# Two heads' scores and values of three attention branches alternate in pinned runs of matmuls, and the compression sums stand in four column groups

## The chip, the cores and the metric

One core of one Trainium2 chip runs the whole program. The metric is the device time of one execution in microseconds (us). Before the change it was 1890.36 us, the median of 3 runs (1888.82 to 1891.26).

TensorE (PE) multiplies a stationary operand, which it loads first, with a moving one. VectorE (DVE), ScalarE (ACT) and GpSimd (POOL) work beside it, and SyncE (SP) issues the transfers. [...]

## The reference

A decoder of two layers on 256 tokens of width 1024. Each layer has four token mixers, a merge of them, and a channel mixer (a dense SwiGLU in layer 0, eight experts of which each token takes two in layer 1). What the change touches, cut to the core:

```
# A: per head, three groups g of banded attention over 256 keys, mixed by their softmax sums
#    (three groups' exponentials over one common sum)
# C: per query head, three attentions with a sigmoid gate each:
kc = gelu(flat(k_cmp blocks) @ w1[0] + b1[0]) @ w2[0] + b2[0]     # compression, 15 blocks, K = 2048
vc = gelu(flat(v_cmp blocks) @ w1[1] + b1[1]) @ w2[1] + b2[1]
o  = g0*softmax(q kc^T) vc + g1*softmax(q k_slc^T) v_slc + g2*softmax(q k_win^T) v_win
# D: sliding window of 128 keys, 6 query heads on 2 key heads, a learned sink in the denominator
o_d = softmax(q k^T) v * sigmoid(lse - sink)
# each branch (256 x 384) then: merged += sigmoid(x @ w_gate + b) * (branch @ w_branch)
```

## The kernel before, in words

Tokens are handled in two tiles of 128 rows (`t` = 0 and 1), and features in tiles of 128. A head has 64 features, so one feature tile holds two heads: head s = 0 in its rows 0 to 63, s = 1 in rows 64 to 127 (`half`, L267).

**Projections.** Every weight tile (128x1024) is loaded by SP (L77), copied in reduced precision by ACT and completed by a DVE subtraction (`split_into`, L81), and used in 24 matmuls of 256 columns (`mm3`, L95, L97, L103). These go on all through the mixers: q and k for branch A (`z_a`), for the conv, for C and D (`zmm`, `ztile`), then the merge gates (`gates`, L486) and the merges. They read only the layer's input, or branches that are done, so they are the work that fills PE between attention steps.

**Attention.** A unit is one pair of heads `j` and one row tile `t`. It computes scores into a PSUM tile `sc` (two of these exist, 1024 columns each), adds the mask and takes the row extremum (DVE), exponentiates (ACT), takes the reciprocal and scales (DVE), transposes 128x128 blocks on PE (`transposed`, L264), copies them to SBUF as `pt` (ACT), and multiplies them with the values into `po` (one PSUM tile, head s in its rows 64s to 64s+63), which `branch_out` (L232) writes out as two parts. Per layer `attn_a` (L270) has 3 pairs, `attn_c` (L408) 3 and `attn_d` (L305) 3.
In `attn_a` the six score products of t = 0 come head by head (L284), the three of each head at t = 1 in a pass of its own; the value products (L300) come head by head too, with 64 columns of weights. `attn_c` does the same with two score products per head (L425, L426), values of two key sets (L453) and a last product over the 16 compressed blocks (L455), which has 16 rows; these 16 columns are transposed apart (L443) and copied by DVE (L447). `attn_d` issues one score product for each head (L312) and one or two value products for each (L337).

**Compression.** `compress` (L342) sums 16 products of 128x32 weights for k and then 16 for v into 32 partitions (L368), transposes the result in two pieces (L374), and goes on with a gelu.

**Order.** A list scheduler sets each engine's order when the program is built. It takes whatever is ready by its own estimates, so projections stand between attention steps. Before the change nothing binds it in the attention.

Of the kernel before, what the change touches and what calls it, by code (L numbers as in the profile page):

```python
# [41 lines left out]
def build(ctx, tc, d):  # L42
# [121 lines left out]
    with tc.tile_pool(name="psa", bufs=1, space=PSUM) as pa:  # L164
# [4 lines left out]
        def po_ps():  # L169
            return pa.tile([P, 512], F32, tag="po", name="po", bufs=1)  # L170
# [19 lines left out]
        for i in range(DEPTH):  # L190
            with tc.tile_pool(name=f"mix{i}", bufs=1) as mp:
# [77 lines left out]

                def attn_a(j, br):  # L270
                    for t in range(NT):
                        nk = (t + 1) * P
                        n = 3 * nk
                        po = po_ps()
                        mask = (ma0 if t == 0 else ma1).rearrange("p g n -> p (g n)")
                        for heads in (((0, 1),) if t == 0 else ((0,), (1,))):
                            ps = sc_ps()
# [17 lines left out]
                            for b, s in enumerate(heads):  # L295
                                for g in range(3):
                                    for kb in range(t + 1):
                                        c = (g * 6 + 2 * j + s) * 64
                                        o = b * n + g * nk + kb * P
                                        te.matmul(po[half(s), :P], vt[:, kb, c:c + 64], pt[:, o:o + P],  # L300
                                                  start=(g + kb == 0), stop=(g == 2 and kb == t))
                        branch_out(po[:, :P], br[j][0][:, t * P:(t + 1) * P], br[j][1][:, t * P:(t + 1) * P], 0.5)


                def attn_d(br, zq, zk):  # L305
                    for j in range(3):
                        for t in range(NT):
                            nk = (t + 1) * P
                            po = po_ps()
                            ps = sc_ps()  # L310
# [1016 lines left out]
```

## Time and profile before

| | us |
|---|---|
| median of 3 runs | 1890.36 |
| the profiled execution | 1891.61 |
| its span from first to last instruction | 1889.6 |
| PE busy | 1808.7 (96%) |
| PE weight loads busy | 1315.5 (70%) |
| DVE busy | 911.8 (48%) |
| ACT busy | 736.0 (39%) |

The span is 2.0 us short of the execution's own time. PE's busy time counts overlapping matmuls once, and the end of each is modelled. So how many run at once is read from the starts in the timeline, not from the busy share. An fp32 product stands there as two records, a projection or a transpose as one. The first 345 us and those from about 635 to 965 us are the two layers' mixers; the experts' stage runs from about 1010 us to the end.

### The profile page before, as it was taken

How to read it: one execution, taken by the hardware profiler on the slowest of the kernel's cores; microseconds unless marked ns; L12 is line 12 of the kernel's file. 1: busy time of each engine (PE TensorE's matmuls, PEld its weight loads, DVE VectorE, ACT ScalarE, POOL GpSimd, SP SyncE). 2: the span in 40 equal slices, each digit the busy share in tenths (PEclk: the TensorE clock that was granted, in tenths of full speed). 3: DMA queues.
4: the chain of work that ended last, by engine and by line, in shares of the span. 5: the costliest groups of instructions: out<-in, count | busy, mean ns of one | idle time of the engine just before them, and what ended most of it. 6: DMA issues, size and time to landing. Idle time of an engine off the chain costs nothing. (4 is left out here: it accounts for less than half of the span.)

```text
span 1889.6 us, 28149 instructions
## 1 busy us (share of the span) xinstructions
PE 1808.7 (96%) x11091; PEld 1315.5 (70%) x11091; DVE 911.8 (48%) x1565; ACT 736.0 (39%) x1185; POOL 78.1 (4%) x115
## 2 busy tenths in 40 slices
PE   8999999999999999999999999999999998998995
PEld 8998789979998999878997454434554453454341
DVE  5565565767555556555577433313333341333232
ACT  4444554545443344455453333213233241233220
POOL 2000001300001000000220000000000000000000
PEclk9999999999999999999999999999999999999998
DMA  7434235567554334423557999999999999999995
GB/s 252 149 141 161 74 137 183 194 219 256 194 185 161 134 134 157 157 72 115 189 201 300 382 421 421 421 421 421 421 421 421 421 421 421 421 420 421 422 421 211
DMA packets 99516, 524.10 MB, mean 277 GB/s; under 512 B 11696, under 2 KB 12464, under 8 KB 56368
## 3 DMA queue, kind: packets, MB, share of 16 engines
q1 hardware_dynamic: 99376, 522.22, 70.5%
q8 instruction: 89, 1.46, 0.3%
q14 instruction: 51, 0.42, 0.1%
HBM read 519.03 MB, written 3.15 MB: 276 GB/s over the span
## 5 line engine op out<-in xcount | busy, mean ns | idle before, releaser
L81 DVE TENSOR_TENSOR wl<-raw,wh 128x1024 fp32r<-128x1024 f32 (+3 forms) x325 | 396.5, 1227 | 211.6 <-ACT wh L81 163.2
L81 ACT CAST wh<-raw 128x1024 fp32r<-128x1024 f32 (+3 forms) x325 | 329.1, 1020 | 347.8 <-PE mm L97 202.4
L95 PE MATMUL mm<-xth,wh 128*128 128x256 f32 x1472 | 363.7, 285 | 5.8 <-ACT wh L81 5.8
L97 PE MATMUL mm<-xtl,wh 128*128 128x256 f32 x1472 | 361.1, 283 | 0.0
L95 PEld LDWEIGHTS mm<-xth,wh 128*128 128x128 f32 x1472 | 278.8, 189 | 13.5 <-ACT wh L81 6.3
L97 PEld LDWEIGHTS mm<-xtl,wh 128*128 128x128 f32 x1472 | 278.8, 189 | 5.3 <-issue 3.4
L1030 PE MATMUL mm<-mraw,xes 128*64 128x512 f32 x1024 | 238.2, 599 | 13.0 <-DMA mraw<-in_mgu 9.8
L103 PE MATMUL mm<-xth,wl 128*128 128x256 f32 x1472 | 212.3, 283 | 0.0
L103 PEld LDWEIGHTS mm<-xth,wl 128*128 128x128 f32 x1472 | 189.3, 190 | 4.6 <-issue 3.9
L1039 DVE TENSOR_TENSOR hsm<-hsm,mm 64x512 f32<-64x512 f32 x42 | 28.5, 678 | 310.6 <-ACT hsm L1038 310.6
L1030 PEld LDWEIGHTS mm<-mraw,xes 128*64 128x64 f32 x1024 | 67.3, 136 | 151.1 <-issue 118.3
L81 DVE TENSOR_TENSOR wl<-mraw,wh 128x1024 fp32r<-128x1024 f32 x118 | 138.8, 1221 | 41.9 <-ACT wh L81 40.5
L81 ACT CAST wh<-mraw 128x1024 fp32r<-128x1024 f32 x118 | 118.6, 1049 | 41.6 <-DMA mraw<-in_mgu 29.4
L1038 ACT ACTIVATE hsm<-mm 64x512 f32<-64x512 f32 x42 | 24.9, 593 | 272.5 <-PE mm L1030 272.5
L1061 PE MATMUL sc<-mraw,hts 128*64 128x512 f32 x472 | 110.2, 597 | 10.1 <-ACT hsm L1038 3.2
L892 PE MATMUL mm<-wh,xth 128*128 128x512 f32 x224 | 96.5, 431 | 14.9 <-ACT wh L81 14.9
L893 PE MATMUL mm<-wh,xtl 128*128 128x512 f32 x224 | 88.6, 396 | 0.0
L1061 PEld LDWEIGHTS sc<-mraw,hts 128*64 128x64 f32 x472 | 32.0, 136 | 80.7 <-issue 60.7
L501 POOL TENSOR_TENSOR x<-x,gt 128x256 f32<-128x256 f32 x48 | 50.1, 1064 | 665.6 <-DVE gt L499 665.6
L1030 PE MATMUL mm<-raw,xes 128*64 128x512 f32 x320 | 75.3, 599 | 2.4 <-DMA raw<-in_mgu 2.3
L896 PE MATMUL mm<-wl,xth 128*128 128x512 f32 x224 | 71.4, 400 | 0.6
L892 PEld LDWEIGHTS mm<-wh,xth 128*128 128x128 f32 x224 | 42.4, 189 | 35.7 <-ACT wh L81 26.9
(341 smaller groups left out, 2439.4 us busy)
## 6 DMA issues: line engine op xcount, KB each, us to landing
mraw<-in_mgu SPq DMA_DIRECT2D x166, 1024.0 KB, 19.8
mraw<-in_md SPq DMA_DIRECT2D x80, 1024.0 KB, 19.8
raw<-in_mgu SPq DMA_DIRECT2D x58, 1024.0 KB, 19.8
raw<-in_wz SPq DMA_DIRECT2D x75, 512.0 KB, 4.1
raw<-in_wmg SPq DMA_DIRECT2D x64, 512.0 KB, 4.3
raw<-in_md SPq DMA_DIRECT2D x32, 1024.0 KB, 19.8
raw<-in_wv SPq DMA_DIRECT2D x24, 520.0 KB, 4.5
raw<-in_wbr SPq DMA_DIRECT2D x32, 384.0 KB, 3.5
```

Source lines behind the costliest of these rows:

```text
L81: return sc.copy(hi, src), v.tensor_tensor(lo, src, hi.bitcast(F32), ALU.subtract)
L95: te.matmul(ps, ah[asl], bh[bsl], start=first, stop=False)
L97: te.matmul(ps, ah[asl], bl[bsl], start=False, stop=False)
L103: te.matmul(ps, lhs, rhs, start=False, stop=last)
L501: gp.tensor_tensor(merged[j], merged[j], gs[j], ALU.add)
L892: mm(ps, ah[asl], bh[bsl], start=first, stop=False)
L893: mm(ps, al[asl], bh[bsl], start=False, stop=False)
L896: mm(ps, lhs, rhs, start=False, stop=last_)
L1030: mm(ps[HP * s:HP * s + HP], self.xe[:, k], w[s][cols(a * 512, 512)], start=(k == 0), stop=(k == KD - 1))
L1038: sc.activation(h[:HP], ps[HP:], AF.Silu)
L1039: v.tensor_tensor(h[:HP], h[:HP], ps[:HP], ALU.mult)
L1061: mm(self.dn[HP * c:HP * c + HP], ht[:, a], w[cols(c * 512, 512)], start=(n == 0), stop=(n == 4 * NFB - 1))
```

## The change

- `together` (new) issues a list of products and ties each behind the one before it on PE, so that they stand in one run; with `behind` the first is tied to what was traced before it.
- Scores (`attn_a`, `attn_c`, `attn_d`): the products of the two heads alternate, s = 0, 1, 0, 1, in the two row halves, into different banks. At t = 1 both heads' scores come in one run, before either head's softmax. From a unit's second row tile on (in C and D also from the second pair on) they are tied behind the unit before's values.
- Values (`pv`, new): the products of both heads alternate in the two column halves, in one run once both heads' `pt` are there. `po` holds both row tiles of a pair, and `branch_out` runs once per pair on 256 columns.
- `attn_d` takes both row tiles in one unit: one softmax tile, six transposes, one copy.
- `attn_c`: the compressed scores go to tiles `pc` of 128 columns, zero behind the 16, and `vc` gets 128 rows, zero below the 16. So the transposes and the last value product have the shape of the others, ACT copies `pt` with them (640 or 768 columns), and the DVE copy is gone.
- `compress`: four sums of eight products (k and v, two halves each) in four groups of 32 columns, one product of each in turn; all four weight tiles are loaded first. One transpose of 128x128, and DVE adds the halves.
- The tag `zc` has 6 buffers, not 8.

```
+def together(products, behind=False):
+    for n, (out, lhs, rhs, first, last) in enumerate(products):
+        ins = te.matmul(out, lhs, rhs, start=first, stop=last)
+        if n or behind:
+            tc.keep_in_program_order(ins)
+def pv(po, t, blocks):
+    todo = [blocks(s) for s in range(2)]
+    together([(po[half(s), t * P:(t + 1) * P], *todo[s][n], n == 0, n == len(todo[s]) - 1)
+              for n in range(len(todo[0])) for s in (1, 0)])
...
 def attn_a(j, br):
+    po = po_ps()
     for t in range(NT):
         nk = (t + 1) * P
         n = 3 * nk
-        po = po_ps()
         mask = (ma0 if t == 0 else ma1).rearrange("p g n -> p (g n)")
-        for heads in (((0, 1),) if t == 0 else ((0,), (1,))):
-            ps = sc_ps()
+        groups = ((0, 1),) if t == 0 else ((0,), (1,))
+        tiles = [sc_ps() for _ in groups]
+        pss = [tiles[0][:, 512 * s:] if t == 0 else tiles[s] for s in range(2)]
+        together([(pss[s][:, g * nk:(g + 1) * nk], za["q", g, j][half(s), t * P:(t + 1) * P],
+                   za["k", g, j][half(s), :nk], True, True) for g in range(3) for s in range(2)], t > 0)
+        where = {}
+        for heads in groups:
             pe = soft_tile()
             nh = len(heads)
             st = sm(3 * nh)
-            for b, s in enumerate(heads):
-                for g in range(3):
-                    o = 512 * b + g * nk
-                    te.matmul(ps[:, o:o + nk], za["q", g, j][half(s), t * P:(t + 1) * P],
-                              za["k", g, j][half(s), :nk], start=True, stop=True)
             spans = [(b * n, n) for b in range(nh)]
             for b, (o, w) in enumerate(spans):
-                v.tensor_tensor_reduce(pe[:, o:o + w], ps[:, 512 * b:512 * b + w], mask, 1.0, 3e38, ALU.add, ALU.min,
-                                       st[:, b:b + 1])
+                v.tensor_tensor_reduce(pe[:, o:o + w], pss[heads[b]][:, :w], mask, 1.0, 3e38, ALU.add,
+                                       ALU.min, st[:, b:b + 1])
             softmax_rows(pe, st, spans)
             scale_rows(pe, st[:, 2 * nh:], spans)
             pst = transposed(pe, 3 * nh * (t + 1))
             pt = pt_tile()
             sc.copy(pt[:, :nh * n], pst[:, :nh * n])
             for b, s in enumerate(heads):
-                for g in range(3):
-                    for kb in range(t + 1):
-                        c = (g * 6 + 2 * j + s) * 64
-                        o = b * n + g * nk + kb * P
-                        te.matmul(po[half(s), :P], vt[:, kb, c:c + 64], pt[:, o:o + P],
-                                  start=(g + kb == 0), stop=(g == 2 and kb == t))
-        branch_out(po[:, :P], br[j][0][:, t * P:(t + 1) * P], br[j][1][:, t * P:(t + 1) * P], 0.5)
+                where[s] = pt[:, b * n:b * n + n]
+        def blocks(s):
+            return [(vt[:, kb, (g * 6 + 2 * j + s) * 64:(g * 6 + 2 * j + s) * 64 + 64],
+                     where[s][:, g * nk + kb * P:g * nk + (kb + 1) * P])
+                    for g in range(3) for kb in range(t + 1)]
+        pv(po, t, blocks)
+    branch_out(po[:, :S], br[j][0], br[j][1], 0.5)
...
 def attn_d(br, zq, zk):
     for j in range(3):
+        po = po_ps()
+        tiles = [sc_ps() for _ in range(NT)]
+        together([(tiles[t][:, 512 * s:512 * s + (t + 1) * P], zq[j][half(s), t * P:(t + 1) * P],
+                   zk[half(s), :(t + 1) * P], True, True) for t in range(NT) for s in range(2)], j > 0)
+        pe = soft_tile()
+        st = sm(12)
...
+        spans = [(0, P), (P, P), (2 * P, S), (2 * P + S, S)]
...
+        pst = transposed(pe, 6)
+        pt = pt_tile()
+        sc.copy(pt, pst[:, :3 * S])
+        for t in range(NT):
+            pv(po, t, lambda s: [
+                (vt[:, kb, 1408 + s * 64:1408 + s * 64 + 64],
+                 pt[:, spans[2 * t + s][0] + kb * P:spans[2 * t + s][0] + (kb + 1) * P])
+                for kb in range(t + 1)])
+        branch_out(po[:, :S], br[j][0], br[j][1], 0.5)
...
-    for kv in range(2):
-        for half in range(2):
-            w = load(d["w1"][i, kv, half], 1024)
-            for a in range(8):
-                b = 8 * half + a
-                te.matmul(ps[:32, kv * P:(kv + 1) * P], gs[kv][:, b].rearrange("p h c -> p (h c)"),
-                          w[:, a * P:(a + 1) * P], start=(b == 0), stop=(b == 15))
-    hs = stile([32, S], F32, "chs", 1, mp)
-    v.tensor_copy(hs, ps[:32, :S])
+    w = [load(d["w1"][i, n // 2, n % 2], 1024) for n in range(4)]
+    together([(ps[32 * n:32 * n + 32, :P], gs[n // 2][:, 8 * (n % 2) + a].rearrange("p h c -> p (h c)"),
+               w[n][:, a * P:(a + 1) * P], a == 0, a == 7) for a in range(8) for n in (3, 2, 1, 0)])
+    hs = stile([P, P], F32, "chs", 1, mp)
+    v.tensor_copy(hs, ps[:, :P])
...
-    for kv in range(2):
-        te.transpose(ps[:, kv * 32:kv * 32 + 32], hs[:, kv * P:(kv + 1) * P], ident[:32, :32])
+    te.transpose(ps[:, :P], hs, ident)
...
     for kv in range(2):
-        v.tensor_scalar(hx[:, kv * 32:kv * 32 + 32], ps[:, kv * 32:kv * 32 + 32],
-                        pp[:, PP_B1 + kv:PP_B1 + kv + 1], None, ALU.add)
+        c = slice(kv * 32, kv * 32 + 32)
+        v.tensor_scalar(hx[:, c], ps[:, kv * 64:kv * 64 + 32], pp[:, PP_B1 + kv:PP_B1 + kv + 1], None,
+                        ALU.add)
+        v.tensor_tensor(hx[:, c], hx[:, c], ps[:, kv * 64 + 32:kv * 64 + 64], ALU.add)
...
-    vc = stile([16, 2, 64], F32, "vc", 1, mp)
+    vc = stile([P, 2, 64], F32, "vc", 1, mp)
+    v.memset(vc, 0.0)
     for hd in range(2):
-        v.scalar_tensor_tensor(vc[:, hd], psv[:16, hd * 64:hd * 64 + 64], 0.5, b2v[:16], ALU.mult,
+        v.scalar_tensor_tensor(vc[:16, hd], psv[:16, hd * 64:hd * 64 + 64], 0.5, b2v[:16], ALU.mult,
...
+    pcs = [stile([P, 2, P], F32, f"pc{n}", 1, mp) for n in range(2)]
+    for pc in pcs:
+        v.memset(pc, 0.0)
     for j in range(3):
+        po = po_ps()
         for t in range(NT):
             nk = (t + 1) * P
...
             mask = ma0[:, 0, :] if t == 0 else mc1
-            for heads in (((0, 1),) if t == 0 else ((0,), (1,))):
+            groups = ((0, 1),) if t == 0 else ((0,), (1,))
+            tiles = [sc_ps() for _ in groups]
+            pss = [tiles[0][:, 512 * s:] if t == 0 else tiles[s] for s in range(2)]
+            wo = 16 + nk if t == 0 else 512
+            together([(pss[s][:, o:o + w], zq[j][half(s), t * P:(t + 1) * P], z[half(s), :w], True, True)
+                      for z, o, w in ((zw, wo, nk), (zs, 0, 16 + nk)) for s in range(2)],
+                     j + t > 0)
+            where = {}
+            pc = pcs[(j + t) % 2]
+            for heads in groups:
                 nh = len(heads)
...
-                    q = zq[j][half(s), t * P:(t + 1) * P]
-                    so = 512 * b
-                    wo = so + (16 + nk if t == 0 else 512)
-                    te.matmul(ps[:, so:so + 16 + nk], q, zs[half(s), :16 + nk], start=True, stop=True)
-                    te.matmul(ps[:, wo:wo + nk], q, zw[half(s), :nk], start=True, stop=True)
...
+                    for dst, src, w, mk in ((pc[:, s, :16], 0, 16, mcmp[:, t, :]),
+                                            (pe[:, o:o + nk], 16, nk, mask),
+                                            (pe[:, o + nk:o + 2 * nk], wo, nk, mask)):
...
+                pst = transposed(pe, 4)
+                for b, s in enumerate(heads):
+                    te.transpose(pst[:, 512 + b * P:512 + (b + 1) * P], pc[:, s], ident)
                 pt = pt_tile()
-                sc.copy(pt[:, :nb * P], pst[:, :nb * P])
-                v.tensor_copy(pt[:16, 512:512 + nh * P], pst[:16, 512:512 + nh * P])
+                sc.copy(pt[:, :512 + nh * P], pst[:, :512 + nh * P])
...
-                    for br_i in range(2):
-                        for kb in range(t + 1):
-                            c = 1152 + br_i * 128 + s * 64
-                            o = 2 * nk * b + br_i * nk + kb * P
-                            te.matmul(po[half(s), :P], vt[:, kb, c:c + 64], pt[:, o:o + P],
-                                      start=(br_i + kb == 0), stop=False)
-                    te.matmul(po[half(s), :P], vc[:, s], pt[:16, 512 + b * P:512 + (b + 1) * P],
-                              start=False, stop=True)
-            branch_out(po[:, :P], br[j][0][:, t * P:(t + 1) * P], br[j][1][:, t * P:(t + 1) * P], 0.25)
+                    where[s] = (pt[:, 2 * nk * b:2 * nk * (b + 1)], pt[:, 512 + b * P:512 + (b + 1) * P])
+            def blocks(s):
+                return [(vt[:, kb, 1152 + br_i * 128 + s * 64:1152 + br_i * 128 + s * 64 + 64],
+                         where[s][0][:, br_i * nk + kb * P:br_i * nk + (kb + 1) * P])
+                        for br_i in range(2) for kb in range(t + 1)] + [(vc[:, s], where[s][1])]
+            pv(po, t, blocks)
+        branch_out(po[:, :S], br[j][0], br[j][1], 0.25)
...
-zw = ztile(Z_CMP + 3, None, "zc", 8)
+zw = ztile(Z_CMP + 3, None, "zc", 6)
...
-zk = ztile(Z_KD, None, "zc", 8)
-zqd = [ztile(Z_KD + 1 + j, NSC, "zc", 8) for j in range(3)]
+zk = ztile(Z_KD, None, "zc", 6)
+zqd = [ztile(Z_KD + 1 + j, NSC, "zc", 6) for j in range(3)]
```

How this moves instructions, in three places. `mm` rows are projections, `za` the q and k of A, `ms` the softmax rows, `pt` their transposes, `vt` the values, `vc` the compressed values, `zc` and `zs` the q and k of C.

PE in layer 0, `attn_a(1)`, t = 1. Before, the first head's transposes, the second head's scores and the first head's values stand in a row:

```order
L97 MATMUL mm<-xtl,wh 128x256
L103 MATMUL mm<-xth,wl 128x256 x4
L264 MATMUL sc<-ident,ms 128x128 x6
L284 MATMUL sc<-za 128x256 x3
L300 MATMUL po<-pt,vt 64x128 x6
L103 MATMUL mm<-xth,wl 128x256 x4
L95 MATMUL mm<-xth,wh 128x256
```

The same unit now, from the second head's transposes to the values of both:

```order
L103 MATMUL mm<-xth,wl 128x256 x2
L264 MATMUL sc<-ident,ms 128x128 x6
L103 MATMUL mm<-xth,wl 128x256 x6
L95 MATMUL mm<-xth,wh 128x256
L97 MATMUL mm<-xtl,wh 128x256
L274 MATMUL po<-pt,vt 64x128 x12
L95 MATMUL mm<-xth,wh 128x256
```

The values of both heads moved into one run of 12 products, 8 projections behind the second head's transposes. The six score products moved to before either head's transposes, right behind the values of t = 0; after them come 21 projections, the first head's transposes, 13 projections and the second head's.

PE in layer 0, `attn_c`, from the second head's transposes at t = 1 of the first pair on. Before:

```order
L264 MATMUL sc<-ident,ms 128x128 x4
L443 MATMUL sc<-ident,ms 16x128
L425 MATMUL sc<-zs,zc 128x144
L426 MATMUL sc<-zc 128x128
L103 MATMUL mm<-xth,wl 128x256 x2
L453 MATMUL po<-pt,vt 64x128 x4
L103 MATMUL mm<-xth,wl 128x256
L95 MATMUL mm<-xth,wh 128x256
L97 MATMUL mm<-xtl,wh 128x256
L455 MATMUL po<-pt,vc 64x128
```

The change, from the run of values on:

```order
L95 MATMUL mm<-xth,wh 128x256
L274 MATMUL po<-pt,vt 64x128 x8
L274 MATMUL po<-pt,vc 64x128 x2
L274 MATMUL sc<-zc 128x128 x2
L274 MATMUL sc<-zs,zc 128x144 x2
L97 MATMUL mm<-xtl,wh 128x256
```

Values of both heads and the next unit's scores are one run. Behind it stand 29 projections before the transposes at t = 0, and 29 (first pair) or 20 at t = 1; in `attn_d` it is 21 to 26.

ACT in layer 0 with the change, in the second pair of `attn_c`: `pc` and `ms` rows are exponentials, `gt` a merge gate.

```order
L470 COPY pt<-sc 128x640 x2
L233 ACTIVATE brh<-po 128x256
L457 ACTIVATE pc_2047,sm_2161<-pc_2047,sm_2161 128x16
L457 ACTIVATE ms,sm_2161<-ms,sm_2161 128x128 x2
L457 ACTIVATE pc_2047,sm_2161<-pc_2047,sm_2161 128x16
L457 ACTIVATE ms,sm_2161<-ms,sm_2161 128x128 x2
L81 CAST wh<-raw 128x1024 x2
L470 COPY pt<-sc 128x768
L509 ACTIVATE gt<-mm,bmh 128x256
```

Two weight casts stand between the exponentials of a unit and the copy of its transposes; the write-out of a pair comes once, before the next pair's exponentials.

## Rows read from the trace of the kernel before

**Rows 1.** The page, busy time by engine: us, share of the span, instructions.
```profile
PE 1808.7 (96%) x11091; PEld 1315.5 (70%) x11091; DVE 911.8 (48%) x1565; ACT 736.0 (39%) x1185; POOL 78.1 (4%) x115
```
**Rows 2.** Busy time by stretch: layer 0's attention, then the experts; columns in its first line.
```profile
core 0: us, PE busy (x) PEld busy (x) DVE busy (x) ACT busy (x) POOL busy (x), PEclk, DMA share, GB/s
60.00:300.00 240.00, 238.69 (x1834) 212.25 (x1833) 138.30 (x382) 119.85 (x264) 0.74 (x1) 1.00 0.37 131
...
1000.00:1890.00 890.00, 824.53 (x3761) 413.25 (x3759) 315.04 (x393) 252.76 (x342) 5.12 (x8) 0.99 0.97 403
```
**Rows 3.** The same view for one pair of A, of C, of D, and compression.
```profile
89.61:110.04 20.43, 20.42 (x155) 17.92 (x154) 11.70 (x24) 9.30 (x16) 0.00 (x0) 1.00 0.28 103
206.62:226.25 19.63, 19.63 (x134) 15.54 (x133) 11.10 (x52) 11.77 (x38) 0.00 (x0) 1.00 0.12 41
252.71:263.06 10.35, 10.17 (x75) 8.03 (x74) 5.97 (x23) 6.26 (x19) 0.00 (x0) 1.00 0.29 101
167.01:175.24 8.23, 7.41 (x67) 7.10 (x66) 2.26 (x4) 2.09 (x2) 0.00 (x0) 1.00 0.57 199
```
**Rows 4.** Timeline of PE, that pair of A: start, length, operation, count.
```profile
90.68 0.94 PE L284 MATMUL sc<-za 64*128 64x128 f32 x8
91.54 0.39 PE L95 MATMUL mm<-xth,wh 128*128 128x256 f32 x1
...
93.30 1.11 PE L103 MATMUL mm<-xth,wl 128*128 128x256 f32 x8
...
94.37 0.84 PE L264 MATMUL sc<-ident,ms 128*128 128x128 f32 x6
95.14 1.56 PE L284 MATMUL sc<-za 64*128 64x256 f32 x6
96.63 1.14 PE L300 MATMUL po<-pt,vt 128*64 128x128 f32 x12
...
108.59 1.52 PE L300 MATMUL po<-pt,vt 128*64 128x128 f32 x12
```
**Rows 5.** Timeline of PE, that pair of D.
```profile
252.71 0.49 PE L312 MATMUL sc<-zc 64*128 64x128 f32 x4
...
253.81 0.67 PE L337 MATMUL po<-pt,vt 128*64 128x128 f32 x8
```
**Rows 6.** Timeline of PE, compression in layer 0.
```profile
167.01 7.17 PE L368 MATMUL mm<-raw,row 128*32 128x128 f32 x64
175.00 0.31 PE L374 MATMUL mm<-ident,chs 32*128 32x32 f32 x2 [0.82 <-DVE chs L371]
```
**Rows 7.** Timeline of DVE and ACT, one head's softmax in A at t = 1.
```profile
102.37 0.96 DVE L288 CUSTOM_DVE_ANT_0 ms<-sc,ma 128x768 f32<-128x768 f32 x1 [2.52 <-PE sc L284]
...
103.38 0.94 ACT L253 ACTIVATE ms<-ms,sm 128x768 f32<-128x768 f32 x1 [1.69 <-DVE sm L288]
...
104.22 0.19 ACT L253 ACTIVATION_READ_ACCUMULATOR ms<-ms,sm 128x1 f32 x1
...
106.03 0.61 DVE L259 TENSOR_SCALAR ms<-ms,sm 128x768 f32<-128x768 f32 x1
```
**Rows 8.** Timeline of DVE, one head's softmax in C at t = 1: first and last.
```profile
218.99 0.17 DVE L431 CUSTOM_DVE_ANT_0 ms<-sc,mcmp 128x16 f32<-128x16 f32 x1
...
221.09 0.76 DVE L259 TENSOR_SCALAR ms<-ms,sm 128x16 f32<-128x16 f32 x3
```
**Rows 9.** Groups by line: busy us, mean ns of one, idle before and its releasers.
```profile
L81 DVE TENSOR_TENSOR wl<-raw,wh 128x1024 fp32r<-128x1024 f32 (+3 forms) x325 | 396.5, 1227 | 211.6 <-ACT wh L81 163.2 <-PE mm L103 43.0 <-ACT sm L326 4.6
...
L81 ACT CAST wh<-raw 128x1024 fp32r<-128x1024 f32 (+3 forms) x325 | 329.1, 1020 | 347.8 <-PE mm L97 202.4 <-PE mm L100 37.1 <-PE sc L100 34.7
...
L294 ACT COPY pt<-sc 128x768 f32<-128x768 f32 x18 | 14.4, 799 | 9.8 <-PE sc L264 9.6
...
L323 ACT ACTIVATE ms<-ms,sm 128x128 f32<-128x128 f32 (+1 forms) x24 | 10.7, 447 | 0.9 <-DVE sm L321 0.5
...
L446 ACT COPY pt<-sc 128x512 f32<-128x512 f32 x18 | 10.5, 585 | 18.4 <-PE sc L443 17.9
```
**Rows 10.** Timeline of SP around the start of the experts' loads.
```profile
1003.23 5.43 SPq L634 DMA_DIRECT2D pw_dram<-pt  x4
...
1013.71 2.41 SPq L874 DMA_DIRECT2D mraw<-in_mgu  x4
```

More of the change, by code (lines that the diff above doesn't have):

```diff
@@ new lines, in attn_d @@
+                        for b, (o, w) in enumerate(spans):
+                            t, s = divmod(b, 2)
+                            h = 3 * s + j
+                            v.tensor_tensor_reduce(pe[:, o:o + w], tiles[t][:, 512 * s:512 * s + w],
+                                                   ma0[:, 0, :] if t == 0 else md1, 1.0, nsk[:, h:h + 1], ALU.add,
+                                                   ALU.min, st[:, b:b + 1])
+                            sc.activation(pe[:, o:o + w], pe[:, o:o + w], AF.Exp, bias=st[:, b:b + 1], scale=-1.0,
+                                          accum_out=st[:, 4 + b:5 + b])
@@ new lines, in attn_d @@
+                        for t in range(NT):
+                            v.tensor_tensor(es[:, 2 * t:2 * t + 2], st[:, 2 * t:2 * t + 2], small[:, 64 + j:68 + j:3],
+                                            ALU.add)
+                        sc.activation(es, es, AF.Exp)
+                        v.tensor_tensor(es, es, st[:, 4:8], ALU.add)
+                        v.reciprocal(st[:, 8:12], es)
+                        scale_rows(pe, st[:, 8:12], spans)
+                        pst = transposed(pe, 6)
@@ L427, in attn_c @@
                                     o = 2 * nk * b
-                                    for do, w, src, mk in ((oc + 16 * b, 16, so, mcmp[:, t, :]), (o, nk, so + 16, mask),
-                                                           (o + nk, nk, wo, mask)):
+                                    for dst, src, w, mk in ((pc[:, s, :16], 0, 16, mcmp[:, t, :]),
+                                                            (pe[:, o:o + nk], 16, nk, mask),
+                                                            (pe[:, o + nk:o + 2 * nk], wo, nk, mask)):
@@ L435, in attn_c @@
-                                r = st[:, 6 * nh:9 * nh]
+                                        spans.append(dst)
+                                n = len(spans)
+                                for c, span in enumerate(spans):
+                                    sc.activation(span, span, AF.Exp, bias=st[:, c:c + 1], scale=-1.0,
+                                                  accum_out=st[:, n + c:n + c + 1])
+                                v.reciprocal(st[:, 2 * n:3 * n], st[:, n:2 * n])
@@ L436, in attn_c @@
+                                r = st[:, 2 * n:3 * n]
                                 for b, s in enumerate(heads):
@@ L438, in attn_c @@
                                     v.tensor_tensor(rb, rb, gt[:, t, :, 3 * s + j], ALU.mult)
-                                scale_rows(pe, r, spans)
-                                nb = 2 * (t + 1) * nh
-                                pst = transposed(pe, nb)
-                                for b in range(nh):
-                                    te.transpose(pst[:16, 512 + b * P:512 + (b + 1) * P], pe[:, oc + 16 * b:oc + 16 * b + 16],
-                                                 ident)
+                                for c, span in enumerate(spans):
+                                    v.tensor_scalar(span, span, r[:, c:c + 1], None, ALU.mult)
@@ L571, in build @@
                 zs = ztile(Z_CMP + 2, None, "zs", 1, 16, 272)
-                zw = ztile(Z_CMP + 3, None, "zc", 8)
+                zw = ztile(Z_CMP + 3, None, "zc", 6)
                 next(cmp)
-                zqc = [ztile(Z_QC + j, NSC, "zc", 8) for j in range(3)]
+                zqc = [ztile(Z_QC + j, NSC, "zc", 6) for j in range(3)]
                 psk, vc = next(cmp)
```

41 lines of the change are left out of this document (3 added, 38 removed).

## The prediction

> **What bounds the kernel now.** First the page: PE is busy 96% of the span, DVE 48%, ACT 39% [rows 1]. Then the table by stretch [rows 2]. [...] In the experts' stretch DMA is at 0.97 and sets the pace. So time that PE saves in the mixers counts, if PE stays fed there and if the experts' loads start earlier. They do: SP issues them at 1013.7, right behind the write-out of layer 1's mixer phase at 1003 [rows 10].
>
> Next, the same table cut to one pair of heads of each branch [rows 3]. Only projections and attention stand in it. A projection takes 0.119: from 93.30 to 94.37 there are nine starts [rows 4]. A's pair lasts 20.43 and holds 155 records; 78 are attention and one lies over the edge, so 76 projections. They take 9.04, which leaves 11.39 for attention and the changes of shape around it. C: 134 less 64, less two at the edges, is 68, and 19.63 - 8.09 = 11.54. D: 75 less 26 and one is 48, and 10.35 - 5.71 = 4.64. Compression lasts 8.23.
>
> Last, the timeline of PE, for how records overlap. A run's length includes the tail of its last record, so it costs its length less 0.07: the scores at 90.68 are 0.94 long, and the next row begins 0.86 after their start [rows 4]. Six records of one head with 256 columns cost 1.49 (95.14), twelve value records of one head 1.45 (108.59). But eight score records at 90.68, two of head 0 beside six of head 1, cost 0.86, and D's eight value records of two heads cost 0.60 where twelve of one cost 1.45 [rows 4, 5]. So the halves of the array work at the same time where both heads' products are within reach: two streams cost what one does. A stream's step is 0.11 (64 records in 7.17) [rows 6], 0.22 for 256 columns.
>
> **The change part by part.**
> *A, per pair.* Scores t = 0: both streams from the start, 0.86. Values t = 0: six records a stream, D's 0.60 plus two steps, 0.82, where 1.07 is paid now. Scores t = 1: 1.49 for both heads instead of twice. Values t = 1: 1.45 instead of twice. The 18 transposes stay, 0.77 for six at 94.37 with the change of shape behind them, 0.65 without: 1.95. Leaving the projections' shape and coming back costs about 0.2 each time, since the first of them takes 0.22 and the entry 0.09 more; values and scores now lie in one run, so three times: 0.6. Sum 7.17; saved 4.22.
> *C, per pair.* Scores t = 0: D's 0.42 (252.71 [rows 5]) and two steps of 0.12, 0.66. Scores t = 1: four of A's six long records, 1.1. Values t = 0 with the compressed product, now of the same shape, six records a stream: 0.82; t = 1 ten a stream: 1.25. The 16 transposes keep their number: 1.75. Two excursions, 0.4. Sum 5.98; saved 5.56.
> *D, per pair.* Scores 0.42 + 2 x 0.22 = 0.86, values six records a stream 0.82, six transposes 0.65, one excursion 0.2. Sum 2.53; saved 2.11.
> *Compression, twice.* 64 records in four streams are 16 steps, 1.75. The wait for the copy of the sums (0.82 [rows 6]), the transpose and the changes of shape come to some 1.35. So 3.1 instead of 8.23: 5.1. No row shows four groups at once; two at a time would cost 3.5, one 7.0. I take four, since halves already run without loss, and keep the 1.75 per layer for the range.
> Six pairs of each and two compressions: 6 x (4.22 + 5.56 + 2.11) + 10.2 = **81.5 us** less of PE time.
> *Edits that I cost at nothing.* Write-outs are half as many, and the DVE copy of 16 rows goes; DVE and ACT are not the bound. The zeroing of `vc` and `pc` stands at the head of DVE's list. ACT's wider copies lie between 0.585 and 0.799 [rows 9], 0.2 more at most; that is in the waits below. `zc` with 6 buffers: D's later q tiles wait for scores of C's first pairs, long past by then. The four compression loads are a matter of SP; it issues them long before the sums, and if that cover failed, PE would wait for the fourth load instead of the first.
>
> *New waits.* Both heads' scores now stand before either softmax, and the next unit's scores behind the values of this one. So the softmax is covered only by the projections put behind the scores; PE waits in order, with all later projections queued behind the transposes. A, t = 1: mask and exponentials run from 102.37 to 104.41, reciprocal and scaling take 0.61 and about 0.25 more [rows 7], with 0.1 at the start 3.0. 21 projections give 2.6. Wait 0.4, and 0.1 to 0.2 before the values, where eight projections and the change of shape face a copy of 0.8: 0.6 a pair. C, t = 1: 2.86 from the first mask to the last scaling [rows 8], 3.0 with the start, against 2.5 of 20 projections; 0.5. A weight cast (1.02) or split (1.23) can fall into the chain, being in the same queues [rows 9]; I count 1.0 of that a pair, together 1.5. D: four exponentials of 0.447 with their reads, some 2.2, two rounds on DVE and one on ACT around them, 3.6; 21 to 26 projections give 2.6 to 3.2; 0.8. That is 2.9 x 6 = 17. Bounds: nothing, if the schedule's slack is as good as now; and one cast in each of the 30 units more, 17 + 31 = 48, if it is not. I take 17, nearest to rows 7 and 8, which show the chain itself.
>
> 81.5 - 17 = 64.5 off the profiled execution's 1891.6 gives **1827 us**. That execution is 1.2 above the median of the runs, which changes nothing here.
>
> [...] Rows 5 show both heads' value products, in column halves, at one head's pace. [...]
>
> **The rivals.**
> 1. *The softmax chain sets the pace.* Between two runs of a unit ACT must do all exponentials and a copy, and in C it is already busy 11.8 of 19.6 us [rows 3], which the change squeezes into some 16. For it: two casts stand before a copy in ACT's order. Against: PE now hardly waits at the same queues. One cast per unit costs 48 in waits: 1858.
> 2. *Slower: casts and splits in front of every unit.* Place: PE at the first transposes of each unit, tied behind scores that are tied behind values. It decides at 81.5 / 30 = 2.7 us of wait per unit. With two casts and a split in each chain, 3.3 us, it is 98: 1908. Against: PE could then not fill with the projections behind, but the list puts 20 to 29 before each transpose, which cover all but some 0.5.
> 3. *Column halves do not pair in longer runs.* The values of A (0.25 + 1.45 a pair) and C (some 1.7) and compression (5.1 a layer) would gain nothing, 31 in all: 1858. [...] Against it: rows 5.
> 4. *The gain does not arrive*, because the experts' loads keep their start or their pace swallows it: 1890. Against: rows 10 put their start behind the mixer.
>
> **How the numbers follow.** The forecast has 0.76, rival 1 has 0.12, rival 2 0.06, rival 3 0.02, rival 4 0.04. No new waits at all would give 1810, and the forecast's own range is 1809 to 1843. To hold 8 in 10 I go on into rival 1, to 1854; beyond it lie half of rival 1, and rivals 2, 3 and 4, 0.18. A measurement of this kernel can tell about 0.2%, some 4 us, from no change. Faster by more: the forecast and rivals 1 and 3, 0.90. Within: rival 4, 0.04. Slower: rival 2, 0.06.
>
> **What would show it.** In the profile after, one score or value run of a t = 1 unit of A should cost about 1.5 for both heads, C's values about 1.25, compression's records about 1.9 us. The granted clock should stay at 1.00. Idle PE before transposes should add to some 17 us in both layers. SP should start the experts' loads some 65 us earlier, and the experts' stretch keep its length. The step is wrong if runs of both heads cost twice one head's (rival 3), if waits for DVE or ACT before L264 grow to 50 (rival 1) or past 80 (rival 2), or if the loads' start moves and the end doesn't (rival 4).

## The result, and the profile after the change

The changed kernel takes 1827.01 us, the median of 4 runs (1826.12 to 1827.46), where the kernel before takes 1890.81 beside it (4 runs, 1888.82 to 1892.12). The ratio is 0.9663, with a 95% interval of 0.9646 to 0.968. Forecast were 1827 and a range of 1809 to 1854. The profiled execution took 1826.12 with a span of 1824.3, 65.3 less than before.

The page, busy time by engine (answers to [rows 1]):

```profile
PE 1738.2 (95%) x11089; PEld 1269.7 (70%) x11089; DVE 902.9 (49%) x1527; ACT 729.3 (40%) x1155; POOL 78.1 (4%) x115
```

Busy time by stretch: layer 0 up to 300 us, a pair of A, of C, of D, compression, and the experts (answers to [rows 2, 3]):

```profile
core 0: us, PE busy (x) PEld busy (x) DVE busy (x) ACT busy (x) POOL busy (x), PEclk, DMA share, GB/s
60.00:300.00 240.00, 235.49 (x2103) 220.70 (x2102) 152.63 (x381) 131.94 (x269) 10.03 (x10) 1.00 0.45 156
86.27:103.87 17.60, 17.00 (x158) 15.23 (x158) 11.96 (x26) 9.09 (x16) 0.00 (x0) 1.00 0.34 122
185.46:201.14 15.68, 15.15 (x138) 13.54 (x138) 10.34 (x47) 11.31 (x34) 0.00 (x0) 1.00 0.21 78
223.40:230.62 7.22, 6.98 (x62) 6.01 (x61) 4.45 (x19) 5.15 (x15) 0.00 (x0) 1.00 0.47 148
156.90:159.50 2.60, 2.13 (x67) 1.74 (x66) 0.72 (x2) 0.00 (x0) 0.00 (x0) 1.00 0.00 0
935.00:1824.30 889.30, 825.13 (x3760) 414.76 (x3758) 315.07 (x393) 252.43 (x342) 5.12 (x8) 0.99 0.97 404
```

PE is still the bound of the mixers, at granted clock 1.00. In 240 us it now gets through 2103 records, not 1834, and idles 4.5 us instead of 1.3. The experts' stretch starts earlier and keeps its length and its DMA share of 0.97.

Timeline of SP at the start of that stretch (answers to [rows 10]):

```profile
938.05 5.56 SPq L657 DMA_DIRECT2D pw_dram<-pt  x4
...
948.52 5.06 SPq L897 DMA_DIRECT2D mraw<-in_mgu  x7
```

Write-out and loads both stand 65.2 us earlier than before. The end moved by 65.3, so the whole gain was made in the mixers and passed through.

Timeline of PE in that pair of A, then C, D and the compression (answers to [rows 4, 5, 6]):

```profile
86.28 1.17 PE L274 MATMUL sc<-za 64*128 64x128 f32 x12
87.38 0.39 PE L95 MATMUL mm<-xth,wh 128*128 128x256 f32 x1
...
92.36 0.88 PE L274 MATMUL po<-pt,vt 128*64 128x128 f32 x12
93.16 1.57 PE L274 MATMUL sc<-za 64*128 64x256 f32 x12
94.66 0.38 PE L95 MATMUL mm<-xth,wh 128*128 128x256 f32 x1
...
97.05 0.28 PE L95 MATMUL mm<-xth,wh 128*128 128x256 f32 x1
97.79 0.85 PE L264 MATMUL sc<-ident,ms 128*128 128x128 f32 x6 [0.46 <-DVE ms L259]
...
101.81 1.53 PE L274 MATMUL po<-pt,vt 128*64 128x128 f32 x24
103.27 0.39 PE L95 MATMUL mm<-xth,wh 128*128 128x256 f32 x1
...
185.47 1.09 PE L274 MATMUL po<-pt,vt 128*64 128x128 f32 x16
186.39 0.39 PE L274 MATMUL po<-pt,vc 128*64 128x128 f32 x4
186.71 0.49 PE L274 MATMUL sc<-zc 64*128 64x128 f32 x4
...
223.41 0.88 PE L274 MATMUL po<-pt,vt 128*64 128x128 f32 x12
224.21 0.93 PE L274 MATMUL sc<-zc 64*128 64x128 f32 x8
...
157.03 1.96 PE L274 MATMUL mm<-raw,row 128*32 128x128 f32 x64
159.45 0.33 PE L385 MATMUL mm<-ident,chs 128*128 128x128 f32 x1 [0.47 <-DVE chs L383]
```

From a row's start to the next row's start: twelve long score records of both heads cost 1.50 (93.16 to 94.66), 24 value records 1.46 (101.81 to 103.27), which is what one head's six and twelve cost before. C's values cost 1.24 (185.47 to 186.71). The 64 compression records last 1.96, not 7.17. The first transposes at t = 1 now wait for the scaling: 0.74 from the projection at 97.05, where 0.12 is the step of projections.

To see the whole, I sorted the time from each PE record's start to the next one's by the kinds of the two records, from the first score to the last value of each layer. "Product" is a score, a value or any matmul of the compression, its transposes included; us per layer, mean of both layers, with the number of steps. The two last columns are kernels told of below.

| step | before | after | turns off (e4) | heads apart (e12) |
|---|---|---|---|---|
| product to product | 54.6 (405) | 29.0 (435) | 42.3 (433) | 43.1 (427) |
| into and out of a run of products | 23.2 (106) | 10.5 (43) | 11.5 (48) | 14.4 (59) |
| projection to transpose | 4.3 (24) | 9.6 (30) | 10.4 (31) | 7.9 (31) |
| between transposes, and back to projections | 10.5 (95) | 11.8 (120) | 11.8 (119) | 11.3 (112) |
| projection to projection | 124.0 (1009) | 116.4 (947) | 115.6 (945) | 125.7 (1022) |

Two thirds of what is gained, 25.6 us a layer, lie inside the runs; 12.7 come from having 22 runs instead of 53. 5.3 are given back in front of transposes, 1.3 in and behind them. The last line falls because 62 projections moved out of the stretch.

### The profile page after: what moved, and what is told of

Same layout as the page of the kernel before. It is cut to its first block, busy times and chain, and to the rows that moved or that the text cites. A ratio compares the mean times of both kernels' runs of the same rounds, so it can differ in the third digit from the quotient of the medians.

```text
span 1824.3 us, 28048 instructions
## 1 busy us (share of the span) xinstructions
PE 1738.2 (95%) x11089; PEld 1269.7 (70%) x11089; DVE 902.9 (49%) x1527; ACT 729.3 (40%) x1155; POOL 78.1 (4%) x115
## 3 DMA queue, kind: packets, MB, share of 16 engines
q8 instruction: 89, 1.46, 0.3%
## 5 line engine op out<-in xcount | busy, mean ns | idle before, releaser
L524 POOL TENSOR_TENSOR x<-x,gt 128x256 f32<-128x256 f32 x48 | 50.1, 1065 | 600.9 <-DVE gt L522 600.9
```

The source lines that it names most:

```text
L524: gp.tensor_tensor(merged[j], merged[j], gs[j], ALU.add)
```

## Experiments

Eleven kernels ran, each beside the kernel before on the same chip. Ratios go by that, with 95% intervals; the changed kernel has 0.9663.

**Turns inside the runs.** Three kernels each take the turns out of one kind of product; a fourth takes out all.

```
e1 (values)   -  for n in range(len(todo[0])) for s in (1, 0)])
              +  for s in (1, 0) for n in range(len(todo[0]))])
e2 (scores, the same in C and D)
              -  for g in range(3) for s in range(2)], t > 0)
              +  for s in range(2) for g in range(3)], t > 0)
e3 (sums)     -  for a in range(8) for n in (3, 2, 1, 0)])
              +  for n in (3, 2, 1, 0) for a in range(8)])
e4            e1, e2 and e3
```

> The changed kernel, with one edit: within each pinned run of value products all of head 1 come first, then all of head 0, instead of in turn. Theory (column halves work at the same time, so a run costs what one head costs): each run becomes a single stream at 0.11 us a record. A: t = 0 12 records 1.45 instead of 0.82, t = 1 24 records 2.77 instead of 1.46. C: +0.64 and +1.08, D: +0.6. That is 4.3 us for the three units of one j, times 6, 25.6 us: 1853 us (1848 to 1857). The wait before the values is unchanged, since they follow the same copy. Rival (column halves share all rows of the array and never overlap; the values gained from standing in one run): 1827 us, and a run of 24 records keeps its 1.46.

Measured: 1840.06 us, ratio 0.9737 (0.9721 to 0.9753). 13 to 14 more, half of what the theory wanted; the rival's 0 is out too.

> The changed kernel, with one edit: within each pinned run of scores all of head 0 come first, then all of head 1, in A, C and D. Theory (row halves work at the same time): A t = 0 costs 1.45 instead of 0.87 to 1.10, t = 1 2.9 instead of 1.49; C +0.45 and +0.9, D +0.6; 3.85 for the units of one j, times 6 is 23 us. Against it stands that head 0's scores are ready before the run ends, so the first wait for its softmax in A at t = 1 (0.6 us, six times) can shrink: up to 3.7 us back. 1848 us (1844 to 1852). Rival (the order inside a run is worth nothing, the gain is in fewer and longer runs): 1827 us or, with the earlier softmax, 1823.

Measured: 1836.09, ratio 0.9716 (0.9699 to 0.9732). 9 to 10 more, again half.

> The changed kernel, with one edit: the compression's four sums, in their four column groups, come one after the other, eight products each, instead of one product of each in turn. Theory (four column groups work at the same time): 64 records at 0.11 us cost 7.1 instead of about 1.9, 5.1 us more in each layer: 1837 us (1835 to 1839). Rival (the gain there was the single transpose and the one copy, which stay): 1827 us. If only two groups ran at once, the run with turns would have cost 3.5 and this one would add 3.6 a layer: 1834.

Measured: 1831.73, ratio 0.9692 (0.9676 to 0.9708). About 5 more, again half.

> The changed kernel with all three edits at once: values, scores and compression sums are issued group by group, nothing in turn. Everything else of the change stays (pinned runs, one write-out a pair, 128-row shapes in C, both row tiles of D in one unit). Theory (alternation alone carries the gain): 25.6 + 23 + 10.2 = 59 us, less up to 4 for the earlier softmax: 1883 us (1878 to 1888), about 7 below the kernel before, which is what pinning, merged write-outs and equal shapes are worth less the waits they bring. Rival (pinning, shapes and merging carry it): 1827 to 1835 us. A sum well short of the three single edits would mean that part of the alternation only fills time in which PE waits anyway.

Measured: 1855.46, ratio 0.9816 (0.98 to 0.9833). The single edits add up (14 + 10 + 5.5 = 29.5 against 28.9), but to a little under half of the gain. So turns carry some 29 us and the rest, 35, stays without them: both readings were wrong. The runs show why. Timeline of PE with the turns off, A's values at t = 1 (e1):

```profile
103.56 2.46 PE L274 MATMUL po<-pt,vt 128*64 128x128 f32 x24
105.94 0.38 PE L95 MATMUL mm<-xth,wh 128*128 128x256 f32 x1
```

A's scores at t = 1 (e2):

```profile
93.79 2.10 PE L274 MATMUL sc<-za 64*128 64x256 f32 x12
```

and the compression's sums one after the other (e3):

```profile
156.56 5.95 PE L274 MATMUL mm<-raw,row 128*32 128x128 f32 x64
```

The values take 2.38 to the next start, where one stream would take 2.77 (an estimate: 1.45 for twelve records and twelve steps of 0.11). The sums last 5.95, where one stream lasts 7.17 [rows 6]. How late each second stream began follows from these rows and the single records of the kernel before:

- Values: 2.46 less 1.52 for twelve records of one head [rows 4], 0.94. In the row at 108.59 [rows 4] the ninth of twelve starts after 0.92 (the text of the next experiment says tenth).
- Scores: 2.10 less 1.56 for six records of one head [rows 4], 0.54. In the row at 95.14 [rows 4] the third of six starts after 0.54.
- Sums: a third of 5.95 less 1.94 for sixteen records, 1.34. In the row at 167.01 [rows 6] the thirteenth starts after 1.33.

So in all three the second stream began when three records of the part in front had not yet started. The kernel before shows the same directly: its program lists A's values at t = 0 head by head, and in the row at 96.63 [rows 4] the second head's first record starts at 96.906, behind the third of the first head's six (96.900) and ahead of its fourth (97.009). All six units of this kind have it 0.275 behind the first.

**How fine must the turns be?** If the second stream begins there too when three records of the block in front are left, as in these rows, blocks of b records make it b - 4 steps of 0.109 late (the step of the sums, 64 records in 7.17 [rows 6]): not at all for two products (four records), two steps for three.

```
-  for n in range(len(todo[0])) for s in (1, 0)])
+  for b in range(0, len(todo[0]), 2) for s in (1, 0)
+  for n in range(b, min(b + 2, len(todo[0])))])      (e11: 3 for 2)
```

> The changed kernel, with one edit: in the runs of value products the heads take turns by two products instead of one. The runs with heads one after the other showed how far PE works ahead: the first record of the second half starts when three records before it have not started yet (A t = 1: 2.38 instead of 2.77, the second head's first record beside the tenth of twelve). Theory (a record may start up to three records ahead, if its half of the array is free): two products are four records, so the other half's block starts with the second record of this one; a run of 24 records costs 1.46 to 1.50 as before: 1827 us (1825 to 1830). Rival (only the very next product can run beside, so turns must be single): the run of 24 costs 2.0 or more, and the time is 1833 or more.

Measured: 1827.23, ratio 0.9669 (0.9653 to 0.9685).

> The same with turns of three products. Theory (three records ahead): a block is six records, the other half starts two steps late, 0.22, once in a run. A t = 1: 1.68 instead of 1.46; t = 0 of A and C has only three products a head, so this is head by head there and costs 0.27; C t = 1 0.22, D hardly anything: 1.0 for the units of one j, 6 us in all: 1833 us (1830 to 1836). Rival (what counts is only that both heads stand within one run): 1827 us.

Measured: 1833.09, ratio 0.97 (0.9684 to 0.9716). Timeline of PE, A's values at t = 1 in turns of two (e10):

```profile
102.46 1.58 PE L274 MATMUL po<-pt,vt 128*64 128x128 f32 x24
```

and of three (e11):

```profile
103.42 1.80 PE L274 MATMUL po<-pt,vt 128*64 128x128 f32 x24
```

Against 1.53 with single turns these are 0.05 and 0.27 more, and 0.93 without turns. That estimate gives 0, 0.22 and 0.87 (eight steps); for the sums three times twelve steps, 3.92, where 3.99 was measured (5.95 less 1.96). For the scores with heads one after the other (e2) it gives two steps of 0.22, 0.44, where 0.53 was measured (2.10 less 1.57).

**Heads apart.** At t = 1 of A and C each head gets its scores and its values in runs of its own, as before the change. The edit in A, in its main lines; C has the same.

```
...
 for heads in groups:
+    scores(heads, t > 0 and heads[0] == 0)
...
+    if t:
+        pv_of(po, heads[0], blocks)
...
-pv(po, t, blocks)
+if t == 0:
+    pv(po, t, blocks)
```

> The changed kernel, with one part undone: at t = 1 of A and C the two heads have their score runs and value runs apart, each head's scores before its own softmax and its values behind its own transposes, as before the change; inside such a run there is only one head. Runs at t = 0, D, the compression, shapes and write-outs stay as changed; the run count rises from 44 to 60. Theory (each half of the array then works alone): A +1.5 for scores, +1.45 for values, +0.2 for the further run, C +0.95, +1.2, +0.2, in 6 units each, 33 us; the first head's softmax has more projections behind it, which gives back up to 5: 1855 us (1850 to 1861). Rival (heads apart keep PE fed better, and its look-ahead finds the other head anyway): 1840 us or less.

Measured: 1860.19, ratio 0.9841 (0.9825 to 0.9858). 33 more: half of the whole gain is that at t = 1 both heads stand in one run. This must not be added to the 29 us of the turns, since heads that stand apart can't take turns either. Timeline of PE (e12):

```profile
103.00 0.85 PE L264 MATMUL sc<-ident,ms 128*128 128x128 f32 x6
103.78 1.56 PE L274 MATMUL sc<-za 64*128 64x256 f32 x6
105.27 1.52 PE L274 MATMUL po<-pt,vt 128*64 128x128 f32 x12
106.72 0.50 PE L103 MATMUL mm<-xth,wl 128*128 128x256 f32 x2
```

One head's six score and twelve value records cost 1.49 and 1.45, as much as both heads' twelve and 24. So in these runs one half worked at a time. By the table the steps inside runs cost 14.1 a layer more than in the changed kernel and those at their edges 3.9; the waits before transposes fall by 1.7.

**Ties.** The first score product of a unit is not tied behind the values of the unit before.

```
-  if n or behind:
+  if n:
```

> The changed kernel, with one edit: a unit's first score product is no longer tied behind the values of the unit before; the rest of each run stays tied. In the new order of PE the first score product of most units moves up between the transposes of the unit before, and the rest stays behind the values: 64 runs of scores and values instead of 44 in both layers. Theory (PE pays for every change of shape and for every product that stands alone): 20 runs more at 0.17 for the two changes of shape and about 0.2 for the product without a partner, 7 us: 1834 us (1829 to 1838). Rival (tying is a burden, since scores that may go earlier shorten the waits for the softmax): those waits, 12 us in sum in the changed kernel, halve: 1821 us.

Measured: 1834.62, ratio 0.9706 (0.969 to 0.9722). Timeline of PE, A (e6):

```profile
90.55 0.85 PE L264 MATMUL sc<-ident,ms 128*128 128x128 f32 x6
91.33 0.70 PE L274 MATMUL sc<-za 64*128 64x256 f32 x2
91.95 0.38 PE L95 MATMUL mm<-xth,wh 128*128 128x256 f32 x1
...
92.62 0.88 PE L274 MATMUL po<-pt,vt 128*64 128x128 f32 x12
93.43 1.56 PE L274 MATMUL sc<-za 64*128 64x256 f32 x10
```

The stray product costs 0.62 (91.33 to 91.95), and the run that it left is as long with ten records as with twelve, since head 1's stream still has its six.

The time is as the theory said, but one part of the rival came true beside it: the waits before transposes did halve. Further on in the same unit (e6):

```profile
97.31 0.28 PE L95 MATMUL mm<-xth,wh 128*128 128x256 f32 x1
97.64 0.85 PE L264 MATMUL sc<-ident,ms 128*128 128x128 f32 x6
```

The step into the transposes is 0.33 here, where the changed kernel has 0.74, with 21 projections in front in both: head 0's stream has one product less in the run and is done earlier. At t = 1 of C's last two pairs PE's order has 29 projections in front for 20. Over both layers these waits fall from 12.0 to 5.7 us, counted as what each step from a projection to a transpose takes beyond 0.12. So strays and broken runs cost some 14 us, twice what the theory counted, and 6 come back in shorter waits; that the sum came out at 7 is luck.

**Shape.** In C the last value product takes the 16 rows that are not zero.

```
-  + [(vc[:, s], where[s][1])]
+  + [(vc[:16, s], where[s][1][:16])]
```

> The changed kernel, with one edit: in C the last value product of each head takes only the 16 rows that are not zero, of weights and of moving data, as before the change. Theory (a step into another shape costs PE about 0.1 more than a step inside one; the kernel before shows 0.20 into the 16-row products and 0.20 out of them): 12 runs of values with one more change of shape, 0.1 to 0.2 each, 1 to 2.5 us: 1828 to 1830, seen in the trace as runs of 2.0 to 2.1 instead of 1.90. Rival (the equal shape is what let C's runs become so short): 0.4 or more a run, 1832 or more.

Measured in one run: 1829.73. The trace has 2.02 to 2.06 for its runs against 1.88 to 1.91, 0.145 twelve times, 1.7 us. So the equal shape of this product is worth that much by itself and no more; that of the transposes was not tried apart.

**What sets the waits.** First the scores of the next unit go in front of the values, behind the first value product. The edit in A, in its main lines; C and D have the like.

```
-pv(po, t, blocks)
+values = value_products(po, t, blocks)
+if t == 0:
+    pss, products = scores(1)
+    values[1:1] = products
+together(values)
...
```

> The changed kernel, with the order inside a run turned round: behind the first value product come the next unit's scores (within a pair in A, all units in C and D), then the rest of the values. So the next softmax starts 0.7 to 1.3 us earlier against PE. Theory (the wait before the transposes is the difference between the softmax chain and what the list scheduler allows for it, whatever stands in between): the order of PE has 6 projections fewer between that run and the transposes (15 for 21 in A, 14 for 20 in C, 17 for 21 to 24 in D), the same time as the values that now cover the chain. The waits stay: 1827 us (1823 to 1830). Rival (the chain itself sets the wait, a constant time behind the scores, so that whatever starts it earlier ends the wait earlier): the 12 us of waits before transposes fall to 4 or less, 1819 us.

Measured: 1831.03, ratio 0.9691 (0.9675 to 0.9707). Timeline of PE, A (e8):

```profile
93.31 0.43 PE L274 MATMUL po<-pt,vt 128*64 128x128 f32 x2
93.67 1.57 PE L274 MATMUL sc<-za 64*128 64x256 f32 x12
95.17 0.87 PE L274 MATMUL po<-pt,vt 128*64 128x128 f32 x10
...
98.30 0.52 PE L264 MATMUL sc<-ident,ms 128*128 128x128 f32 x3 [0.30 <-DVE ms L259]
```

Against the run's start the scores end 0.44 earlier (1.86 for 2.30), and so do the transposes start (4.99 for 5.43): the chain behind the scores takes the same 3.13. But six projections fewer stand in it, and the wait only shrank from 0.46 to 0.30, in both layers by 1.2 us. So in this unit the chain does end a constant time behind the scores, as the rival says, but its shorter waits are out: the schedule puts fewer projections in front, and PE has next to nothing of the earlier start. The time lies 1 us above the theory's range: it left out that a run which goes from values to scores and back changes shape once more, 2.66 for a run of 2.30.

Then the softmax chain is made longer by a second pass of every scaling. The edit for A and D, in its main lines; C has the like.

```
     v.tensor_scalar(pe[:, o:o + w], pe[:, o:o + w], f[:, b:b + 1], None, ALU.mult)
+for b, (o, w) in enumerate(spans):
+    v.tensor_scalar(pe[:, o:o + w], pe[:, o:o + w], 1.0, None, ALU.mult)
...
```

> The changed kernel with a longer softmax chain: every scaling by the reciprocal is followed by a second pass over the same columns that multiplies by 1.0. That is 0.6 to 0.8 us more of DVE's time in each of 42 chains of both layers (A nine, C nine, D three a layer). Theory (projections cover the chain because the list scheduler counts it, and only what it undercounts is a wait): PE's order has 5 to 16 projections more before the first transposes of a unit (37 for 21 in A at t = 1, 25 for 20 in C, 32 for 21 in D), 0.6 to 1.9 us of cover for 0.6 to 0.8 of chain; the waits before transposes do not grow, and in A at t = 1 and in D they go: 1823 us (1819 to 1830). Rival (the softmax chain sets the pace once both heads' scores stand ahead of it): 42 x 0.65 = 27 us, 1854.

Measured: 1828.41, ratio 0.9673 (0.9657 to 0.969), no different from the changed kernel. DVE is busy for 20.9 us more (923.8), and nothing of it shows in the time: the schedule covered it. But the waits that were to go stayed, 0.40 in A at t = 1 (e9):

```profile
100.07 0.85 PE L266 MATMUL sc<-ident,ms 128*128 128x128 f32 x6 [0.40 <-DVE ms L261]
```

So in these two kernels the schedule fills the chain as far as it reckons it, and falls short by about the same, 0.3 to 0.5 us in these rows, whether the chain is longer or starts earlier. It is no constant: without the ties (e6) the same waits were half as long.

None of these kernels beats the changed one; e10 equals it. Not tried apart: D's two row tiles in one unit, the halved write-outs and the one shape of C's transposes.

## Why the prediction was right

By its own steps. The table has the time that a pair's scores, values, transposes and changes of shape take, waits included. It is a pair's length less 0.119 for each projection in it: in A from the score run to the end of the last values, for all six pairs, in C and D from one pair's run to the next one's, for the middle pair of each layer. The waits are those of the second pair in layer 0.

| us | forecast | of it waits | measured | of it waits before transposes |
|---|---|---|---|---|
| A, a pair | 7.77 | 0.6 | 7.88 to 8.46, mean 8.23 | 0.85 |
| C, a pair | 7.48 | 1.5 | 6.88, 6.86 | 0.84 |
| D, a pair | 3.33 | 0.8 | 3.06, 3.06 | 0.47 |
| compression | 3.1 | | 2.6 | |
| a layer, in all | 58.6 | 8.5 | 58.8, 58.2 | 6.4, 5.6 |

The last line is the stretch of the table of steps, 177.56 and 176.94 us less 998 projections, beside half of the forecast's 17 in waits. Before, the same reckoning gives 90.7 and 90.3 (216.85 less 1060 projections, 216.52 less 1061), against the forecast's 90.9. The stretches so give 64.0 us of the 65.3.

- *Durations of runs.* All held but one: t = 1 scores 1.50 and values 1.46 for both heads, C's values 1.24, D's run 1.66 (0.86 + 0.82 forecast), the sums 1.96. A's scores at t = 0 cost 1.10 in five of six pairs, not 0.86. There the run's third group waits for the copy of its k tile, which DVE does from 86.39 on for 0.42 in the pair shown; tied products can't let a projection past. 0.24 five times is 1.2 us.
- *New waits.* 17 us were forecast; 12.0 stand before transposes (2.9 before the change, counted alike, so 9 new). The profile's own idle time before L264 is less, 5.6 us (0.5 before the change, 1.1 without the ties), since it begins only at the modelled end of the last projection. C was set too high by 0.66 a pair. In the pair of the table no cast and no split stands in a chain. The casts come behind the last exponentials, where only a copy could wait for them, and at t = 0 ACT is idle even before that copy:

```profile
189.94 2.09 ACT L81 CAST wh<-raw 128x1024 fp32r<-128x1024 f32 x2
192.33 0.80 ACT L470 COPY pt<-sc 128x768 f32<-128x768 f32 x1 [0.31 <-PE sc L468]
```

D was too high by 0.33, A too low by 0.25. Against the waits, PE's own work in a layer came out higher, 52.5 where the forecast has 50.1. Among what had no term are A's score wait, and C's first scores and D's last values, which stand in runs of their own. So both layers' waits came 5 us lower than forecast and their work 5 us higher. That the sum was right to 1 us is in this part luck.

- *Rivals.* 1 and 2 wanted waits of 48 or more; 12 came. A chain longer by 21 us of DVE work cost nothing (e9), because projections are put in front of the transposes by the length that the schedule expects. 3 wanted no pairing of column halves: in one run 24 records of both heads cost 1.46, where twelve of one cost 1.45, and the 64 records in four column groups last 1.96, not 7.17. Before the change the pairing was there too: D's eight value records of two heads cost 0.60 [rows 5], where eight of one stream would take 1.45 less four steps, 1.01. 4 fell with the experts' loads, 65.2 us earlier.
- *What the prediction did not see.* It charges every run as if both heads work side by side from the start, where their products are "within reach", and has no term for how far that reaches. The theory of the first four runs went further and took the turns for the whole cause. A little over half of the gain needs none (e4): without turns the time inside the runs is still 12.3 us a layer less than before, since two heads in one run overlap by three records (in e1 the second begins after 0.94, the ninth of twelve after 0.92), and the fewer edges give 11.7. What must not be lost is that both heads stand in the same run (33 us at t = 1 of A and C) and that the turns are no longer than two products: turns of two left 1827.23 (e10), turns of three 1833.09 (e11).

## What to carry to other kernels

Products that use different halves or column groups of the array ran at the same time here: the 24 value records of both heads cost 1.46 in turns of one fp32 product and 1.51 in turns of two (e10), where twelve of one head cost 1.45, and 64 records in four column groups lasted 1.96 for 7.17. In turns of three the 24 cost 1.73 (e11). Put both streams in one run, wait for the later of the two inputs once, and fill the wait with independent matmuls; here that paid 64 us, with 9 more in waits already taken off. When a sum of terms comes out right, still undo one part at a time: here that showed that the turns were half of it.

## What was not expected of the hardware

- PE's records did not all start in the order in which the program lists them. In the kernel before, A's values at t = 0 are listed head by head, yet the second head's first record starts at 96.906, ahead of the first head's fourth, fifth and sixth (97.009, 97.118 and 97.227). By the lengths above it was three records too from one column group to the next (e3, 1.34 a sum) and between row halves (e2, 0.54).
- Four column groups of 32 cost as little here as one: 64 records last 1.96 us. From the first record's start to the last one's are 1.68 (157.03 to 158.71), where the first sixteen of the one stream before the change take 1.66 (167.01 to 168.68).
- One product (two records) of another shape at the head of a run cost about 0.36 by itself (e8, 93.31 to 93.67), and a single stray score product 0.62 (e6, 91.33 to 91.95), with the steps into and out of their shape.
